# A head's RMS-norm factor: from a 128x256 square root and reciprocal to two columns of logarithm, exponential and Newton step

## The chip, the core and the metric

The kernel runs on one core of one Trainium2 chip. The metric is the device time in microseconds, the median of several executions. All times below come from the profiled execution of the kernel before, unless they are called the median of the runs.

The engines are named as in the profile: PE is TensorE, PEld its weight loads, DVE is VectorE, ACT is ScalarE, POOL is GpSimd, SP is SyncE, which issues the DMAs.

## The reference

One layer of a hybrid block over 256 latent tokens and 256 context tokens, model width 2048, all in float32. What matters here is differential attention: 8 heads, each with two query/key halves of 64 channels and 128 value channels, whose output is RMS-normalised per token over its 128 channels.

```python
def diff_attn_core(q, k, v, lam):
    s = jnp.einsum('bqhcd,bkhcd->bhcqk', q, k).astype(jnp.float32) * (ATTN_HEAD_DIM ** -0.5)
    p = jax.nn.softmax(s, axis=-1)
    a = p[:, :, 0] - lam * p[:, :, 1]
    return jnp.einsum('bhqk,bkhe->bqhe', a.astype(v.dtype), v)

def diff_attn_readout(o, subln_w, lam_init):
    B, T = o.shape[0], o.shape[1]
    return (rms_norm(o, subln_w) * (1.0 - lam_init)).reshape(B, T, ATTN_WIDTH)
```

Beside it stands a gated linear recurrence (8 heads, forward and backward) whose gates need a sigmoid, a logarithm and many exponentials. Both branches are merged, projected and added to the residual; a gated MLP with a width-3 convolution follows.

## The kernel before, in words

Channels lie on the 128 partitions and tokens on the free axis. Every product is made of three float32r products (high x high, high x low, low x high). A weight chunk of 128x1024 is loaded (`raw`, 4 buffers), rounded to `whi` by ACT (L72) and its rest put into `wlo` by DVE (L73); `mm3` (L77 to L79) and `gemm2_unit` (L126, L127) are the matmuls. So each weight chunk costs ACT and DVE about a microsecond each, beside whatever a head asks of them.

The stages follow one another: modulation and the first projections up to 145 us, attention from there to about 430 us, the recurrence to about 770 us, then merge, output projection and the MLP. In the stages of the mixers a projection for the next head is computed while the last heads are worked on: a head is a Python generator that yields the number of ticks after which its next part is to be emitted. A chunk of a context projection is 2 ticks, one of a query projection 1 tick; in attention two heads may be under way at once (`depth[0]` is 2). Ticks also feed a background job: a chunk of the modulation weights is loaded and multiplied and summed by DVE (L345).

The order that this emits is only a priority. The scheduler of the kernel language orders each engine's instructions by priority and by its own estimate of when each is ready, and this order is then fixed in the program; each engine takes its instructions strictly in turn. `keep_in_program_order` marks an instruction that must not be moved ahead of what was emitted before it on its engine.

A head in attention: `scores(0)` and `scores(1)` each make six matmuls into the PSUM tile `S` (L395; one buffer), DVE takes the maxima (L398) and scales them (L399), ACT makes two exponentials from `S` (L402). Since `S` has one buffer, the matmuls of `scores(1)` wait until both exponentials of `scores(0)` have read it. Then values and probabilities are transposed on PE into `tp` (PSUM, two buffers), the output is made into `ops[:, 0]`, ACT copies it to `o` (L438) and squares it to `osq` (L440). Two ticks later comes the norm: PE sums the squares over the channels with a matrix of ones, which spreads the sum over all partitions (L442), ACT takes the square root of 128x256 (L444), DVE the reciprocal of 128x256 (L445) and multiplies `o` by weight and factor (L446); ACT and DVE split the result into `att` (L448, L449). Only the merge, much later, reads `att`.

ACT holds one table set of functions at a time, and a load stands in the program wherever the next function is not in the set held. The square root and the exponential have different sets, so the norm of one head and the exponentials of the next load a table each. In the recurrence each head has a sigmoid (L630), a logarithm (L640) and exponentials (L522 to L525, L549), three sets.

When the last head of attention has ended, its SBUF pool is given back; the first tiles of the recurrence (`fq`, `lb`) lie in that memory and wait for it.

Of the kernel before, what the change touches and what calls it, by code (L numbers as in the profile page):

```python
# [16 lines left out]
P = 128  # L17
# [9 lines left out]
C1 = 3  # L27
BG_ATT0 = 0.5
BG_ATT, BG_REC, BG_MRG = 0.7, 0.1, 0.55
LEVELS = [1, 2, 4, 8, 16, 32, 64, 128]  # L30

_COLS = {}
# [9 lines left out]
def body(ctx, tc, cst_d, sel_d, cb_d, ccol_d, wn_d, xT_d, xc_d, lam_d, rope_d, mask_d, wm_d, wg0_d, win_d, wba_d,  # L42
# [288 lines left out]
    with ExitStack() as esa:  # L331
# [19 lines left out]
        with ExitStack() as es:  # L351
            at = es.enter_context(tc.tile_pool(name="at", bufs=1))
            aps = es.enter_context(tc.tile_pool(name="aps", bufs=1, space=PSUM))
            rope = at.tile([P, 2, T], F32, name="rope")
            dma.dma_start(rope, rope_d)

            ls = at.tile([P, 6], F32, name="ls")
            lj = at.tile([P, 64], F32, name="lj")
            lamt = at.tile([P, 256], F32, name="lamt")
            dma.dma_start(lamt, lam_d)  # L360
            for i in range(2):
                dve.scalar_tensor_tensor(lj, lamt[:, 128 * i:128 * i + 64], 1.0, lamt[:, 128 * i + 64:128 * i + 128],
                                         op0=ALU.mult, op1=ALU.mult, accum_out=ls[:, i:i + 1])
            act.activation(ls[:, 2:4], ls[:, 0:2], AF.Exp)
            dve.tensor_sub(ls[:, 4:5], ls[:, 3:4], ls[:, 2:3])
            dve.tensor_scalar_add(ls[:, 5:6], ls[:, 4:5], -LAM_INIT)
            nlam = ls[:, 5:6]
            subw = at.tile([P, 1], F32, name="subw")
            dve.tensor_scalar_mul(subw, col("subw"), 1.0 - LAM_INIT)

            shuf = [(i + 16) % 32 for i in range(32)]

            def rope_apply(out, src):
                rot = at.tile([P, T], F32, tag="rot", name="rot", bufs=2)
                dve.stream_shuffle(rot, src, shuf)
                t1 = at.tile([P, T], F32, tag="t1", name="t1", bufs=2)
                pool.tensor_tensor(t1, src, rope[:, 0, :], ALU.mult)
                pool.tensor_tensor(rot, rot, rope[:, 1, :], ALU.mult)
                dve.tensor_add(out, t1, rot)

            def head(h, kT, vr, qT):
                yield 3
                aT = at.tile([P, 2, 4, T], F32R, tag="aT", name="aT", bufs=1)
                prob = []

                def scores(m):
                    z = at.tile([P, 8], F32, tag="z", name="z", bufs=4)
                    pp = []

                    S = aps.tile([P, 2, 512], F32, tag="S", name="S")  # L390
                    c_ = slice(m * P, (m + 1) * P)
                    for i, (a, b) in enumerate(((0, 0), (0, 1), (1, 0))):
                        for c in range(2):
                            r_ = slice(64 * c, 64 * c + 64)
                            ins = pe.matmul(S[:, c], qT[r_, a, c_], kT[r_, b], start=i == 0, stop=i == 2)  # L395
                            if i or c:
                                tc.keep_in_program_order(ins)
                    dve.reduce_max(z[:, 0:2], S, axis=AX.X)  # L398
                    dve.tensor_scalar_mul(z[:, 2:4], z[:, 0:2], -0.125)  # L399
                    for c in range(2):  # L400
                        p = at.tile([P, 512], F32, tag="p", name="p", bufs=4)
                        act.activation(p, S[:, c], AF.Exp, bias=z[:, 2 + c:3 + c], scale=0.125,  # L402
                                       accum_out=z[:, 4 + c:5 + c])
                        pp.append(p)
                    dve.reciprocal(z[:, 6:8], z[:, 4:6])
                    dve.tensor_mul(z[:, 7:8], z[:, 7:8], nlam)
                    dve.tensor_scalar(pp[1], pp[1], z[:, 7:8], None, op0=ALU.mult)
                    dve.scalar_tensor_tensor(pp[0], pp[0], z[:, 6:7], pp[1], op0=ALU.mult, op1=ALU.add)
                    prob.append(pp[0])

                def turn(m):
                    tp = aps.tile([P, 4, P], F32, tag="tp", name="tp", bufs=2)
                    for i in range(4):
                        pe.transpose(tp[:, i], prob[m][:, i * P:(i + 1) * P], ident)
                    c_ = slice(m * P, (m + 1) * P)
                    act.copy(aT[:, 0, :, c_], tp)
                    dve.tensor_sub(aT[:, 1, :, c_], tp, aT[:, 0, :, c_].bitcast(F32))

                scores(0)
                yield 2  # L420
                scores(1)
                yield 2
                tp = aps.tile([P, 4, P], F32, tag="tp", name="tp", bufs=2)
                for i in range(4):
                    pe.transpose(tp[:, i], vr[:, i * P:(i + 1) * P], ident)
                vn = at.tile([P, 2, 4, P], F32R, tag="vn", name="vn", bufs=1)
                act.copy(vn[:, 0], tp)
                dve.tensor_sub(vn[:, 1], tp, vn[:, 0].bitcast(F32))
                yield 2
                turn(0)  # L430
                yield 1
                turn(1)
                yield 2
                ops = aps.tile([P, 2, T], F32, tag="o", name="ops")
                for i in range(4):
                    mm3(ops[:, 0], vn[:, 0, i], vn[:, 1, i], aT[:, 0, i], aT[:, 1, i], i == 0, i == 3)
                o = at.tile([P, T], F32, tag="o", name="o", bufs=2)
                act.copy(o, ops[:, 0])  # L438
                osq = at.tile([P, T], F32, tag="osq", name="osq")
                act.activation(osq, ops[:, 0], AF.Square)  # L440
                yield 2
                pe.matmul(ops[:, 1], ones, osq, start=True, stop=True)  # L442
                rs = at.tile([P, 2, T], F32, tag="rs", name="rs")
                act.activation(rs[:, 0], ops[:, 1], AF.Sqrt, bias=epst, scale=1.0 / P)  # L444
                dve.reciprocal(rs[:, 1], rs[:, 0])  # L445
                dve.scalar_tensor_tensor(o, o, subw, rs[:, 1], op0=ALU.mult, op1=ALU.mult)  # L446
                a = big.tile([P, 2, T], F32R, tag="ar", name=f"att{h}", bufs=16)
                act.copy(a[:, 0], o)  # L448
                dve.tensor_sub(a[:, 1], o, a[:, 0].bitcast(F32))  # L449
                att.append(a)  # L450

            for h in range(8):
                bg_rate[0] = BG_ATT0 if h < 2 else BG_ATT
                ks = in_tile(AK + h)
                kf = at.tile([P, 512], F32, tag="kf", name="kf")
                act.copy(kf[:, 256:], ks[:, 256:])
                kr = at.tile([P, T], F32, tag="qkr", name="kr", bufs=2)
                act.copy(kr, ks[:, :256])
                rope_apply(kf[:, :256], kr)
                kT = at.tile([P, 2, 512], F32R, tag="kT", name="kT", bufs=2)  # L460
                act.copy(kT[:, 0], kf)
                dve.tensor_sub(kT[:, 1], kf, kT[:, 0].bitcast(F32))

                vs = in_tile(AV + h)
                if AV + h in g0raw:
                    vr = vs
                else:
                    vr = big.tile([P, 512], F32, tag="ar", name="vr", bufs=16)
                    act.copy(vr, vs)

                qs = in_tile(AQ + h)
                qr = at.tile([P, T], F32, tag="qkr", name="qr", bufs=2)
                fold(qr, qs)
                rope_apply(qr, qr)
                qT = at.tile([P, 2, T], F32R, tag="qT", name="qT", bufs=2)
                act.copy(qT[:, 0], qr)
                dve.tensor_sub(qT[:, 1], qr, qT[:, 0].bitcast(F32))
                start(head(h, kT, vr, qT))

            in_tile_early(RFF + 1)  # L480
            in_tile_early(RFB + 1)
            in_tile_early(RI + 1)
            drain()
# [4 lines left out]
        with ExitStack() as es:  # L488
# [128 lines left out]
            for h in range(8):  # L617
# [9 lines left out]
                rqs = in_tile(RQ + h)  # L627
                fold(kkq[:, 2], rqs)
                act.copy(fq[:, 0], kkq[:, 2])
                act.activation(fq[:, 0:5], fq[:, 0:5], AF.Sigmoid)  # L630
                dve.tensor_mul(kkq[:, 2], kkq[:, 2], fq[:, 0])
                for d in range(2):
                    i_ = d * 8 + h
# [3 lines left out]
                pool.tensor_scalar(kc, f[:, :, T:], -1.0, 1.0, op0=ALU.mult, op1=ALU.add)  # L637
                dve.tensor_scalar(g, f, 2.0 ** -62, None, op0=ALU.max)
                dve.tensor_scalar(f, f, 2.0 ** 62, 1.0, op0=ALU.mult, op1=ALU.min)
                act.activation(fq[:, 1:9], fq[:, 1:9], AF.Ln)  # L640
                dve.tensor_add(g, g, f)
                for d, dst in ((1, PL[:, 0]), (0, PL[:, 1]), (1, PL[:, 2])):
                    dve.tensor_tensor_scan(dst[:, 1:], onet, g[:, d, 0:T], 0.0, op0=ALU.mult, op1=ALU.add)
# [318 lines left out]
```

## Time and profile before

| | |
|---|---|
| median of 3 runs | 1903.94 us (1903.0 to 1904.11) |
| the profiled execution, its own time | 1898.9 us |
| its span, first to last instruction | 1897.1 us |
| mean granted TensorE clock | 0.996 of full speed |
| busy: PE, DVE, ACT, POOL | 1841.9 (97%), 1354.3 (71%), 992.7 (52%), 377.6 us (20%) |

The profiled execution took 1898.9 us, 1.8 us more than its span and 5.0 us less than the median of the runs. The busy shares are means over stages that differ, and a busy PE is not PE at its peak, since the ends of matmuls are modelled. What counts for a change in one stage is the idle time of PE in that stage and what ended it.

### The profile page before, as it was taken

To read this page: it belongs to the slowest core of one execution; us is meant where nothing else is said; L and a number is where in the kernel's file an instruction comes from. 1 tells how busy PE (TensorE), PEld (TensorE's weight loads), DVE (VectorE), ACT (ScalarE), POOL (GpSimd) and SP (SyncE) were. 2 spreads that over 40 slices of the span, in tenths; PEclk is the share of its full clock that TensorE was granted. 3 is DMA by queue.
4 is the path that set the end of the run, shared out by engine and by line. 5 is a ranking of instruction groups with operands and counts; after the bars stand their busy time and mean duration, and the time that the engine had idled before them with its cause. 6 is when DMAs were issued, how large, how long until landed. Compare 5 with 4: busy or idle time off the path is not lost.

```text
span 1897.1 us, 27964 instructions
## 1 busy us (share of the span) xinstructions
PE 1841.9 (97%) x10430; PEld 1555.5 (82%) x10430; DVE 1354.3 (71%) x2130; ACT 992.7 (52%) x1501; POOL 377.6 (20%) x328
## 2 busy tenths in 40 slices
PE   7999999998999999999999999999999999999997
PEld 3777787777788888888888889888888888888886
DVE  4549878888866677977777879767677677654444
ACT  3336445447655556744444556555555555534442
POOL 0002111103223333401110110322222222211111
PEclk9999999999999999999999999999999999999998
DMA  9977665674333334688888865666666666666664
GB/s 374 370 274 248 202 197 186 207 267 145 97 111 113 110 103 122 210 269 273 280 272 272 276 192 183 192 189 190 190 188 191 188 195 187 185 193 187 192 192 123
DMA packets 112360, 385.71 MB, mean 203 GB/s; under 512 B 12384, under 2 KB 16608, under 8 KB 112224
## 3 DMA queue, kind: packets, MB, share of 16 engines
q1 hardware_dynamic: 112224, 383.92, 63.9%
q8 instruction: 82, 1.34, 0.3%
q14 instruction: 54, 0.44, 0.1%
HBM read 381.78 MB, written 2.10 MB: 202 GB/s over the span
## 4 chain that ended last, share of the span: by engine, by line
PE 72%; DMA 11%; DVE 10%; issue 4%; ACT 2%; POOL 0%; DVEq 0%; SPq 0%; ACTq 0%; POOLq 0%
PE macc L126 28%; PE macc L127 14%; DMA raw<-in_wm 8%; PE acc L126 5%; PE acc L78 4%; PE acc L79 4%; PE acc L77 4%; DVE wlo L73 3%; PE acc L127 3%; PE g L177 2%; DMA raw<-in_win 2%; DVE raw L345 2%; PE acc L177 2%; PE nat L177 2%; ACT whi L72 1%
## 5 line engine op out<-in xcount | busy, mean ns | idle before, releaser
L73 DVE TENSOR_TENSOR wlo<-raw,whi 128x1024 fp32r<-128x1024 f32 (+1 forms) x514 | 626.8, 1220 | 240.2 <-ACT whi L72 234.4
L72 ACT CAST whi<-raw 128x1024 fp32r<-128x1024 f32 (+1 forms) x514 | 530.6, 1033 | 469.9 <-PE macc L126 155.5
L126 PE MATMUL macc<-h,whi 128*128 128x512 f32 x1344 | 466.0, 391 | 0.0
L127 PE MATMUL macc<-h,wlo 128*128 128x256 f32 x1344 | 376.3, 280 | 0.0
L126 PE MATMUL acc<-h,whi 128*128 128x512 f32 x896 | 323.6, 402 | 1.1 <-DVE kkq L143 0.7
L126 PEld LDWEIGHTS macc<-h,whi 128*128 128x128 f32 x1344 | 251.3, 187 | 55.1
L127 PE MATMUL acc<-h,wlo 128*128 128x256 f32 x896 | 254.3, 284 | 6.2 <-DVE wlo L73 5.9
L127 PEld LDWEIGHTS macc<-h,wlo 128*128 128x128 f32 x1344 | 254.0, 189 | 0.0
L126 PE MATMUL macc<-f,whi 128*128 128x512 f32 x704 | 244.1, 391 | 0.0
L77 PE MATMUL acc<-h,whi 128*128 128x512 f32 x528 | 211.8, 401 | 0.0
L345 DVE SCALAR_TENSOR_TENSOR raw<-raw,cb 128x1024 f32<-128x1024 f32 x128 | 162.2, 1270 | 67.0 <-DMA raw<-in_wm 66.5
L78 PE MATMUL acc<-h,whi 128*128 128x512 f32 x528 | 207.0, 392 | 0.0
L79 PE MATMUL acc<-h,wlo 128*128 128x512 f32 x528 | 206.7, 391 | 0.0
L126 PEld LDWEIGHTS acc<-h,whi 128*128 128x128 f32 x896 | 169.1, 189 | 39.7 <-PE acc L127 1.0
L127 PE MATMUL macc<-f,wlo 128*128 128x256 f32 x704 | 197.1, 280 | 0.0
L127 PEld LDWEIGHTS acc<-h,wlo 128*128 128x128 f32 x896 | 170.0, 190 | 12.8 <-DVE wlo L73 12.2
L126 PEld LDWEIGHTS macc<-f,whi 128*128 128x128 f32 x704 | 131.6, 187 | 28.9
L842 POOL TENSOR_TENSOR u<-u 128x256 f32<-128x256 f32 x44 | 69.2, 1572 | 328.0 <-DVE u L837 288.0
L127 PEld LDWEIGHTS macc<-f,wlo 128*128 128x128 f32 x704 | 133.1, 189 | 0.0
L77 PEld LDWEIGHTS acc<-h,whi 128*128 128x128 f32 x528 | 99.2, 188 | 21.9 <-issue 2.9
L79 PEld LDWEIGHTS acc<-h,wlo 128*128 128x128 f32 x528 | 99.1, 188 | 21.5 <-issue 0.6
L78 PEld LDWEIGHTS acc<-h,whi 128*128 128x128 f32 x528 | 99.3, 188 | 20.5 <-issue 1.8
(740 smaller groups left out, 2639.0 us busy)
## 6 DMA issues: line engine op xcount, KB each, us to landing
raw<-in_win SPq DMA_DIRECT2D x178, 512.0 KB, 4.3
raw<-in_wup SPq DMA_DIRECT2D x168, 512.0 KB, 3.6
raw<-in_wm SPq DMA_DIRECT2D x128, 512.0 KB, 4.3
raw<-in_wdn SPq DMA_DIRECT2D x80, 512.0 KB, 3.7
nraw<-in_wn SPq DMA_DIRECT2D x64, 512.0 KB, 7.8
raw<-in_wout SPq DMA_DIRECT2D x32, 512.0 KB, 4.4
raw<-in_wba SPq DMA_DIRECT2D x16, 512.0 KB, 4.5
raw<-in_wbr SPq DMA_DIRECT2D x16, 512.0 KB, 4.7
```

The source lines that it names most:

```text
L72: act.copy(hi[:, :n], raw[:, :n])
L73: dve.tensor_sub(lo[:, :n], raw[:, :n], hi[:, :n].bitcast(F32))
L77: pe.matmul(ps, wh, xh, start=first, stop=False)
L78: pe.matmul(ps, wh, xl, start=False, stop=False)
L79: pe.matmul(ps, wl, xh, start=False, stop=last)
L126: pe.matmul(ps, hi[:, c_], xs[k][:, :, :T], start=k == 0, stop=False)
L127: pe.matmul(ps[:, :T], lo[:, c_], xs[k][:, 0, :T], start=False, stop=k == len(xs) - 1)
L177: tc.keep_in_program_order(pe.matmul(*args, **kw))
L345: dve.scalar_tensor_tensor(raw, raw, 1.0, cb[half], op0=ALU.mult, op1=ALU.mult, accum_out=modp[:, t - 32, half:half + 1])
L842: pool.tensor_tensor(cs[1], cs[0], cs[1], ALU.mult)
```

## The change

The norm no longer takes its factor for all 128 partitions. Two matmuls with `osq` as weights and one column of ones put the sums of squares by token: tokens on partitions, one column for each half of 128 tokens. On these 128x2 numbers DVE forms mean plus epsilon, ACT takes the logarithm and the exponential of minus half of it, and DVE makes one Newton step on the result (three small instructions). DVE then scales the identity matrix by each column, which makes two diagonal matrices; one tick later PE multiplies ones by these, which spreads the factors over all partitions into `ops[:, 1]`, and the multiplication of `o` reads them from PSUM. The 128x256 square root and reciprocal go.

Logarithm and exponential lie in one table set, which is now loaded by name: once at the start of attention, and in each head of the recurrence between its sigmoid and its logarithm. The order of ACT's table-bound instructions around these loads is kept.

```diff
+LN_EXP = "natural_log_exp_and_others"
...
+            tc.keep_in_program_order(act.preload_act_table_set(LN_EXP))
...
-            act.activation(ls[:, 2:4], ls[:, 0:2], AF.Exp)
+            tc.keep_in_program_order(act.activation(ls[:, 2:4], ls[:, 0:2], AF.Exp))
...
                 yield 2
-                pe.matmul(ops[:, 1], ones, osq, start=True, stop=True)
-                rs = at.tile([P, 2, T], F32, tag="rs", name="rs")
-                act.activation(rs[:, 0], ops[:, 1], AF.Sqrt, bias=epst, scale=1.0 / P)
-                dve.reciprocal(rs[:, 1], rs[:, 0])
-                dve.scalar_tensor_tensor(o, o, subw, rs[:, 1], op0=ALU.mult, op1=ALU.mult)
+                nt = aps.tile([P, 4, P], F32, tag="tp", name="nt", bufs=2)
+                for m in range(2):
+                    pe.matmul(nt[:, 2, m:m + 1], osq[:, m * P:(m + 1) * P], ones[:, 0:1], start=True, stop=True)
+                r = at.tile([P, 4, 2], F32, tag="r", name="r", bufs=2)
+                dve.tensor_scalar(r[:, 0], nt[:, 2, 0:2], 1.0 / P, EPS, op0=ALU.mult, op1=ALU.add)
+                act.activation(r[:, 1], r[:, 0], AF.Ln)
+                act.activation(r[:, 2], r[:, 1], AF.Exp, scale=-0.5)
+                dve.tensor_mul(r[:, 1], r[:, 2], r[:, 2])
+                dve.scalar_tensor_tensor(r[:, 1], r[:, 1], -0.5, r[:, 0], op0=ALU.mult, op1=ALU.mult)
+                dve.scalar_tensor_tensor(r[:, 3], r[:, 1], 1.5, r[:, 2], op0=ALU.add, op1=ALU.mult)
+                dg = at.tile([P, 2, P], F32, tag="osq", name="dg")
+                for m in range(2):
+                    dve.tensor_scalar(dg[:, m], ident, r[:, 3, m:m + 1], None, op0=ALU.mult)
+                yield 1
+                for m in range(2):
+                    pe.matmul(ops[:, 1, m * P:(m + 1) * P], ones, dg[:, m], start=True, stop=True)
+                dve.scalar_tensor_tensor(o, o, subw, ops[:, 1], op0=ALU.mult, op1=ALU.mult)
...
-                act.activation(fq[:, 0:5], fq[:, 0:5], AF.Sigmoid)
+                tc.keep_in_program_order(act.activation(fq[:, 0:5], fq[:, 0:5], AF.Sigmoid))
...
-                act.activation(fq[:, 1:9], fq[:, 1:9], AF.Ln)
+                tc.keep_in_program_order(act.preload_act_table_set(LN_EXP))
+                tc.keep_in_program_order(act.activation(fq[:, 1:9], fq[:, 1:9], AF.Ln))
```

## Rows read from the trace of the kernel before

**Rows 1.** Windows: attention, start and middle of the recurrence; the columns stand above.

```profile
core 0: us, PE busy (x) PEld busy (x) DVE busy (x) ACT busy (x) POOL busy (x), PEclk, DMA share, GB/s
145.00:430.00 285.00, 272.52 (x1372) 220.18 (x1371) 239.19 (x407) 143.72 (x245) 35.74 (x35) 0.99 0.68 218
430.00:500.00 70.00, 61.13 (x331) 50.62 (x330) 63.02 (x109) 51.58 (x74) 24.84 (x24) 1.00 0.40 121
500.00:740.00 240.00, 239.82 (x1237) 204.69 (x1236) 166.85 (x327) 133.63 (x182) 75.56 (x74) 1.00 0.36 108
```

**Rows 2.** PE's waits in attention: us in total, times, longest.

```profile
PE S L395 <- ACT p L402: 8.2, 7, 2.2
```

**Rows 3.** Timeline of PE, one head: start, us, line, xcount [idle before <-releaser].

```profile
312.41 0.59 PE L442 MATMUL ops<-osq,ones 128*128 128x256 f32 x2
312.94 0.96 PE L395 MATMUL S<-kT,qT 64*128 64x512 f32 x6
...
321.21 0.39 PE L79 MATMUL acc<-h,wlo 128*128 128x512 f32 x1
321.44 0.39 PE L77 MATMUL acc<-h,whi 128*128 128x512 f32 x1
323.39 0.96 PE L395 MATMUL S<-kT,qT 64*128 64x512 f32 x6 [1.57 <-ACT p L402]
```

**Rows 4.** Timeline of DVE, the same head.

```profile
316.37 1.22 DVE L398 TENSOR_REDUCE z<-S 128x2 f32<-128x1024 f32 x1
317.50 1.74 DVE L445 RECIPROCAL rs<-rs 128x256 f32<-128x256 f32 x1
319.16 0.11 DVE L399 TENSOR_SCALAR z<-z 128x2 f32<-128x2 f32 x1
...
319.51 0.48 DVE L446 SCALAR_TENSOR_TENSOR o<-o,subw,rs 128x256 f32<-128x256 f32 x1
```

**Rows 5.** Timeline of ACT, the same head.

```profile
313.49 1.28 ACT L444 ACT_TABLE_LOAD   x1
...
319.35 1.28 ACT L402 ACT_TABLE_LOAD   x1 [3.55 <-DVE z L399]
320.64 0.69 ACT L402 ACTIVATE p<-S,z 128x512 f32<-128x512 f32 x1
```

**Rows 6.** ACT's groups in attention: xcount | busy us, mean ns | idle before.

```profile
L402 ACT ACT_TABLE_LOAD x7 | 9.0, 1283 | 19.6 <-DVE z L399 19.6
L444 ACT ACT_TABLE_LOAD x7 | 9.0, 1283 | 0.1
...
L364 ACT ACTIVATE ls<-ls 128x2 f32<-128x2 f32 x1 | 0.2, 205 | 0.0
```

**Rows 7.** Timeline of PE in the first stage: matmuls of two columns.

```profile
62.45 0.50 PE L177 MATMUL nat<-sel,ns 128*128 128x2 f32 x4
62.81 0.48 PE L177 MATMUL g<-h,whi 128*128 128x512 f32 x1
```

**Rows 8.** Timeline of PE in the recurrence: float32 products of 128x128.

```profile
456.52 0.46 PE L571 MATMUL dc<-E 128*128 128x128 f32 x2 [0.68 <-DVE E L552]
456.81 0.39 PE L572 MATMUL dc<-E 128*128 128x128 f32 x2
```

**Rows 9.** DVE's groups in attention.

```profile
L445 DVE RECIPROCAL rs<-rs 128x256 f32<-128x256 f32 x8 | 14.0, 1745 | 0.0
...
L407 DVE TENSOR_SCALAR p<-p,z 128x512 f32<-128x512 f32 x16 | 8.7, 543 | 0.2
```

**Rows 10.** PE's waits in the recurrence: us in total, times, longest.

```profile
PE ktp L565 <- DVE KQ L526: 2.8, 1, 2.8
PE ktp L565 <- issue: 1.9, 1, 1.9
```

**Rows 11.** Timeline of ACT at the start of the recurrence.

```profile
425.10 0.62 ACT L626 COPY fq<-g0sb 128x512 f32<-128x512 f32 x1 [1.12 <-DVE att L449]
425.74 1.28 ACT L503 ACT_TABLE_LOAD   x1
...
442.10 1.28 ACT L640 ACT_TABLE_LOAD   x1 [0.44 <-DVE fq L639]
```

## The prediction, made before the change was run

> **What bounds the kernel now.** I read the busy time by stretch first, because the change touches two stages only [rows 1]. In attention PE is busy 272.5 of 285 us, so about 12.5 us are idle; DVE is busy 239 and ACT 144. In the first 70 us of the recurrence PE idles 8.9 us, and in the 240 us after that 0.2 us. So the later recurrence is PE's own pace: whatever ACT saves there moves nothing. All that this change can give lies in the 12.5 us of attention and the 8.9 us at the start of the recurrence, and anything it adds to PE has to be paid almost in full.
>
> The waits of PE say what the 12.5 us are [rows 2]: 8.2 us, in seven pieces of at most 2.2, are the scores' matmuls that wait for the exponentials that still read the only `S` buffer. One head shows how that comes about [rows 3 to 5]. The first scores are issued at 312.94. DVE takes their maxima at 316.37, but the scaling of these maxima (0.11 us) comes only at 319.16, because the reciprocal of the norm of the head before stands between them for 1.66 us. Then ACT, idle for 3.55 us until the scaled maxima are there, loads the table of the exponential, 1.28 us, because the square root had loaded its own at 313.49. The exponentials begin at 320.64, and the second scores, next in PE's order, begin at 323.39 after 1.57 us of idle PE. So the reciprocal and one of the two table loads lie on the path that ends in PE's wait; the other load, at 313.49, lies where ACT has slack.
>
> **The change, part by part.** The sum is made against the profiled execution's own 1898.9 us.
>
> *ACT.* Seven loads for the square root and seven for the exponential go [rows 6]; the logarithm and the exponential on two columns cost 0.205 us each, by the 128x2 exponential in the same group. That is 2.57 us less and 0.41 more per head. As total load it is worth nothing, since ACT is busy half of the stage [rows 1]; only the 1.28 us between maxima and exponentials counts.
>
> *DVE.* The reciprocal goes, 1.745 us [rows 9]. In its place come four instructions on two columns. The scaling of the maxima, of the same shape, took 0.11 us [rows 4]; I take 0.16 each, half as much again, since each waits for the result of the one before. Two more make 128x128 from the identity: between 0.11 for 2 columns and 0.54 for 512 [rows 4, 9] a straight line gives 0.22 each. Sum 1.1 us, so 0.6 less per head.
>
> *The wait of the scores.* If the new small instructions stand just where the reciprocal stood, the exponentials start 1.28 + 1.66 - 1.1 = 1.8 us sooner, which covers every wait but the longest. If a staging instruction of about 1.2 us (the length of the maxima in [rows 4]) slips between them as well, it is 0.6 us, times seven 4.3 us. The upper end is the whole 8.2. I take 6.5: nearest to the first case, with some kept back because the first heads have no norm in front of them.
>
> *PE.* The norm's matmul took 0.53 us (312.41 to 312.94, [rows 3]). Now there are two products with the squares as weights and one column to multiply. The trace has the like: two products with two columns, four passes, 62.45 to 62.81, 0.36 us [rows 7]. And two float32 products of 128x128, 0.29 us each (456.52 to 456.81, [rows 8]), 0.58. So 0.36 + 0.58 - 0.53 = 0.41 us more per head, 3.3 over eight; 2.9 if the spreading costs what the old matmul did, 4.1 if each switch costs another 0.1. PE has no slack in this stage, so all of it counts.
>
> *The new wait.* Before, nothing on PE waited for the norm. Now the spreading does, at the end of a chain PE, DVE, ACT twice, DVE five times, PE, and all later matmuls of PE, staged weights or not, queue behind it. The bare chain is 0.4 + 0.15 + 0.4 + 0.4 + 0.45, about 1.8 us, with the queues of DVE (up to two staging instructions) and ACT up to some 6. The cover is what is emitted between the two: six scores matmuls (0.96 us) and one chunk of the next projection, 24 matmuls at 0.23 (321.21 to 321.44), 5.5 us; 6.5 in all. So it is mostly covered, and the scheduler will put it later if it reckons it late. I take 0.8 us over the eight heads, with 0 and 12 (1.5 per head) as ends, because in this very stage the scheduler's estimate left the scores 1 to 2 us short.
>
> *The two other tiles.* The sums borrow a buffer of `tp` and the diagonals the buffer of `osq`. Both are free by then (the transposes of the head are over, the squares read), and read again by the next head only some six ticks later: nothing, unless the spreading is delayed by more than that cover.
>
> *Start of the recurrence.* The first tile there waits for the last head's `att` (425.10, [rows 11]), then comes the table load for the exponential of `lb`, 1.28 us, which goes since that set is already held. The load before the logarithm stood behind the wait for its operand (442.10) and may now be done ahead of it, another 1.28. PE's waits there that hang on this chain are 4.7 us [rows 10]. The last head's norm is also the release of the memory; its chain has more hops but no reciprocal and no loads. I take a gain of 2.0, with 4.7 at the good end and a loss of 3 if the longer chain of hops releases the memory later.
>
> How a load is to be priced can be read twice. In the rows it is 1.28 us and nothing more: the exponential starts at 320.64, where the load that began at 319.35 ends [rows 5]. The Trainium skill, ScalarE: Activation LUTs, What ACT_TABLE_LOAD costs, adds a drain of some 1.38 us to the 1.28, 2.66 for every change of set. By that price, an estimate, the longest wait would go too (0.4 more) and the two loads of the recurrence's start would count double (2.7 more), and the sum below would be about 3 us lower; the trace speaks against it.
>
> **Sum.** -6.5 + 3.3 + 0.8 - 2.0 = -4.4 us: 1894.5 us for an execution like the profiled one, and, as that stood 5.0 us under the median, 1899.5 us as the median. The bound of no change that can be told is 0.2%, 3.8 us.
>
> **The rivals.** *The wait only moves (0.25).* The scores no longer wait, but the spreading does, by about as much: the second scores are emitted right behind it. For it speaks that both hang on the same two queues; against it that the chain has 6.5 us of cover. -6.5 + 3.3 + 4.5 - 0.5 = +0.8: 1904.7 us.
>
> *The spreading matmul becomes a barrier (0.15).* It is the slow side: PE takes its matmuls in turn, and the scores at 323.39 show weights staged and ready matmuls standing behind one that waits [rows 3]. If the chain takes 8 us instead of 6.5 in each head, -6.5 + 3.3 + 12 = +8.8, 1912.7 us. It decides from about 1.1 us per head on (0.1 is in the forecast; 8.2 us more over eight heads make +3.8). The Trainium skill, TensorE: Matmul & The Clock Gate, Step-by-step: what each phase is for, has the same rule, that only weight loads are pulled ahead and matmuls stay in order; the trace agrees, with that 1.57 us.
>
> *All of it is won (0.15).* Scores wait no more (8.2), the spreading is hidden, and the recurrence starts without its 4.7 us: -8.2 + 2.9 - 4.7 = -10.0, 1893.9 us.
>
> *The loads stay (0.05).* If the exponentials of the scores still get a load of their own set, only reciprocal for small instructions is won: 0.56 x 7 = 3.9 against 3.3: 1903.3 us.
>
> **How the numbers follow.** The forecast has 0.40, with its own range of -8 to -1 us around -4.4, 1896 to 1903; some two thirds of it lie beyond -3.8. Faster by over 0.2%: 0.27 of it, 0.15 of all won, 0.03 of the rest, 0.45. Slower: the barrier and a little of the moved wait, 0.17. Within 0.2%: 0.38. The range of 8 in 10 goes from 1892.5, a little beyond all won, to 1908.5, between the moved wait and the full barrier.
>
> **What will show it.** Right: attention's table loads fall from 14 at scores and norm to none, the exponentials start within 1 us of the scaled maxima, PE's wait of the scores falls from 8.2 to under 2, the spreading matmuls wait under 0.3 us each, and the middle of the recurrence keeps its length although its table loads fall too. Wrong: a PE wait of over 1 us at the spreading matmul in most heads; scores that still wait a microsecond, because DVE's order puts something else between maxima and scaling; or a start of the recurrence that comes later because the last norm's hops each queue behind a staged chunk.

## The result, and the profile after

The changed kernel took 1913.17 us (median of 4 runs, 1909.81 to 1914.67) against 1903.47 us of the kernel before on the same chip: a ratio of 1.0052, 95% interval 1.0039 to 1.0065. It is slower by 0.4 to 0.65%; the forecast was 1899.5 us with a range up to 1908.5. The profiled execution has a span of 1911.0 us, 13.9 more than the one before. That is some 4 more than the difference of the medians, 9.7 us, since the profiled execution of the kernel before stood 5.0 us under its median and this one 0.4.

The page's busy times of the changed kernel:

```profile
PE 1851.3 (97%) x10478; PEld 1567.7 (82%) x10478; DVE 1352.3 (71%) x2170; ACT 969.6 (51%) x1491; POOL 382.8 (20%) x328
```

The same line of the kernel before:

```profile
PE 1841.9 (97%) x10430; PEld 1555.5 (82%) x10430; DVE 1354.3 (71%) x2130; ACT 992.7 (52%) x1501; POOL 377.6 (20%) x328
```

ACT lost its 23 us, and the time grew all the same: PE is busy 9.4 us longer and idle (span less busy) 59.7 us instead of 55.2, 4.5 more. That is the whole 13.9.

Both traces hold the same products of the projections (`acc`) in number, so, with their order taken as the same, the n-th of one can be set beside the n-th of the other. By them the changed kernel is 0.4 us ahead where the kernel before stands at 300 us and 4.4 behind at 330; between these lies the head shown below. It is 6.2 behind at 430, 11.2 behind from 520 to 790 and 13.9 at the end of the span.

Windows of the changed kernel, columns as in [rows 1]: attention, three parts of it of 15 us, and the start and middle of the recurrence.

```profile
145.00:430.00 285.00, 271.96 (x1381) 221.56 (x1380) 234.12 (x442) 120.62 (x237) 33.16 (x34) 0.98 0.66 211
165.00:180.00 15.00, 13.07 (x55) 9.82 (x53) 14.26 (x24) 6.28 (x12) 1.42 (x2) 0.89 0.85 273
315.00:330.00 15.00, 11.58 (x44) 8.63 (x44) 13.46 (x28) 4.88 (x13) 1.51 (x2) 0.77 0.44 140
390.00:405.00 15.00, 12.47 (x54) 9.47 (x53) 14.33 (x32) 5.35 (x14) 0.00 (x0) 0.89 0.78 254
430.00:500.00 70.00, 60.50 (x312) 50.89 (x311) 55.83 (x98) 51.55 (x67) 25.90 (x19) 0.94 0.41 127
500.00:740.00 240.00, 239.09 (x1232) 204.20 (x1231) 170.71 (x331) 127.03 (x182) 78.83 (x76) 1.00 0.35 106
```

The column after POOL is the granted clock. In the start of the recurrence it is 0.94 instead of 1.00. A clock of 0.77 over 15 us is 6.9 us at the lower level, 1.2 instead of 2.4 GHz (0.23 x 15 x 2); 0.94 over 70 us is 8.4. Read so all over the span up to its last 50 us, the changed kernel has some 27 us at the lower level, the kernel before 3.3. Of the 27, 13.5 lie in attention, 10.2 at the start of the recurrence and 3.3 in the merge. The middle of the recurrence takes what it took, as forecast.

PE's waits in attention, which answer to [rows 2]:

```profile
PE ops L462 <- DVE dg L459: 8.5, 4, 3.4
PE S L398 <- ACT p L405: 3.0, 2, 1.9
```

The scores wait 3.0 us instead of 8.2. The new spreading matmul (L462) waits 8.5 for the diagonal. Together they are 11.5, more than before; since other small waits went, PE idles 13.0 us in attention against 12.5 by the windows. The head at 312 us, the one of [rows 3 to 5], shows where the new wait arises. PE:

```profile
312.01 0.50 PE L449 MATMUL nt<-ones,osq 128*128 128x1 f32 x4
312.44 0.96 PE L398 MATMUL S<-kT,qT 64*128 64x512 f32 x6
...
318.68 0.39 PE L80 MATMUL acc<-h,wlo 128*128 128x512 f32 x1
322.49 1.22 PE L462 MATMUL ops<-dg,ones 128*128 128x128 f32 x4 [3.42 <-DVE dg L459]
323.64 1.65 PE L398 MATMUL S<-kT,qT 64*128 64x512 f32 x6
325.21 0.79 PE L78 MATMUL acc<-h,whi 128*128 128x512 f32 x1
```

DVE, with the norm's instructions L451 to L459:

```profile
315.66 1.23 DVE L346 SCALAR_TENSOR_TENSOR raw<-raw,cb 128x1024 f32<-128x1024 f32 x1 [4.43 <-DMA raw<-in_wm]
316.81 0.08 DVE L346 DVE_READ_ACCUMULATOR raw<-raw,cb 128x1 f32 x1
316.81 0.15 DVE L451 TENSOR_SCALAR r<-nt 128x2 f32<-128x2 f32 x1
316.89 1.22 DVE L74 TENSOR_TENSOR wlo<-raw,whi 128x1024 fp32r<-128x1024 f32 x1
318.02 0.69 DVE L454 TENSOR_TENSOR r<-r 128x2 f32<-128x2 f32 x1
318.64 1.21 DVE L401 TENSOR_REDUCE z<-S 128x2 f32<-128x1024 f32 x1
...
320.48 1.75 DVE L346 SCALAR_TENSOR_TENSOR raw<-raw,cb 128x1024 f32<-128x1024 f32 x1
322.16 0.08 DVE L346 DVE_READ_ACCUMULATOR raw<-raw,cb 128x1 f32 x1
322.16 0.47 DVE L459 TENSOR_SCALAR dg<-ident,r 128x128 f32<-128x128 f32 x2
```

The reader is to see three things. The sums are on PE from 312.01 to 312.44, but DVE stands for 4.43 us, until 315.66, at L346, a background product (the modulation weights), because that chunk's load has not landed; the norm's first instruction is behind it in DVE's order. Then the chain's small steps are each queued behind a large one: a staging subtraction, the maxima, another background product of 1.75 us. So the spreading starts 10.1 us after the sums, where PE's cover ends at 319.07 (318.68 + 0.39). Of the 10.1, 3.2 are the standing for the load (312.44 to 315.66); the rest are instructions that run. And after 3.42 us of idling PE runs at the lower clock: the spreading takes 1.22 us instead of 0.71 at 262.89, where it waited 1.72 us, the scores 1.65 instead of 0.96, a product 0.79 instead of 0.50.

Over attention DVE stands 22.8 us for such loads:

```profile
DVE raw L346 <- DMA raw<-in_wm: 22.8, 14, 4.6
```

The kernel before has the same wait, and in the same head too, so the change didn't bring it; it put a matmul of PE behind it.

```profile
DVE raw L345 <- DMA raw<-in_wm: 23.0, 17, 4.5
314.08 1.23 DVE L345 SCALAR_TENSOR_TENSOR raw<-raw,cb 128x1024 f32<-128x1024 f32 x1 [4.35 <-DMA raw<-in_wm]
```

### The profile page after: what moved, and what is told of

Read it like the earlier page. It is cut to its first block, busy times and chain, and to the rows that moved or that the text cites. A ratio compares the mean times of both kernels' runs of the same rounds, so it can differ in the third digit from the quotient of the medians.

```text
span 1911.0 us, 28075 instructions
## 1 busy us (share of the span) xinstructions
PE 1851.3 (97%) x10478; PEld 1567.7 (82%) x10478; DVE 1352.3 (71%) x2170; ACT 969.6 (51%) x1491; POOL 382.8 (20%) x328
## 4 chain that ended last, share of the span: by engine, by line
PE 59%; DMA 7%; DVE 5%; issue 2%; ACT 1%; POOL 0%; DVEq 0%; ACTq 0%; POOLq 0%
PE macc L127 28%; PE macc L128 14%; DMA raw<-in_wm 5%; PE acc L79 3%; PE acc L78 3%; PE acc L80 3%; PE acc L127 3%; DVE wlo L74 2%; PE acc L128 2%; DMA raw<-in_win 1%; PE lv L607 1%; DVE raw L346 1%; DMA raw<-in_wba 1%; ACT whi L73 1%; PE stp L598 0%
## 5 line engine op out<-in xcount | busy, mean ns | idle before, releaser
L127 PE MATMUL macc<-h,whi 128*128 128x512 f32 x1344 | 466.0, 391 | 0.0
L127 PE MATMUL acc<-h,whi 128*128 128x512 f32 x896 | 322.9, 401 | 0.0
L127 PEld LDWEIGHTS macc<-h,whi 128*128 128x128 f32 x1344 | 251.3, 187 | 55.1
L127 PE MATMUL macc<-f,whi 128*128 128x512 f32 x704 | 244.1, 391 | 0.0
L346 DVE SCALAR_TENSOR_TENSOR raw<-raw,cb 128x1024 f32<-128x1024 f32 x128 | 160.8, 1260 | 72.4 <-DMA raw<-in_wm 71.9
L127 PEld LDWEIGHTS acc<-h,whi 128*128 128x128 f32 x896 | 169.0, 189 | 37.0 <-issue 0.7
L127 PEld LDWEIGHTS macc<-f,whi 128*128 128x128 f32 x704 | 131.6, 187 | 28.9
```

Of the source, the lines that this page charges most:

```text
L127: pe.matmul(ps, hi[:, c_], xs[k][:, :, :T], start=k == 0, stop=False)
L346: dve.scalar_tensor_tensor(raw, raw, 1.0, cb[half], op0=ALU.mult, op1=ALU.mult, accum_out=modp[:, t - 32, half:half + 1])
```

## The experiments

Ratios are to the kernel before on the same chip. An expectation speaks of theory A: the spreading matmul is late, and all of PE's work behind it; B: the recurrence's half of the change costs; C: the extra matmul work on PE costs it, without any long wait; and of D, formed after the first four runs: DVE's background products, waiting in its order for their loads, delay whatever chain PE waits for.

**The two halves apart.** First the norm's new form with the recurrence as before.

> Only the norm and the table set of attention are changed; the recurrence is left as before. Of the 13.9 us by which the changed kernel's profiled span is longer, 5.6 have arisen by the last head's norm, 3.5 in the recurrence and 4.8 after it. If the late spreading matmul is the cause and the rest only follows from it (theory A): +8 to +12 us over before. If the kept order and the named load in the recurrence cost by themselves (theory B): +4 to +6 us, the attention's share alone. If the extra matmul work is the cause (theory C): +3 us, with no PE wait of over 1 us needed.

Then the recurrence's half alone:

```
-                act.activation(fq[:, 0:5], fq[:, 0:5], AF.Sigmoid)
+                tc.keep_in_program_order(act.activation(fq[:, 0:5], fq[:, 0:5], AF.Sigmoid))
...
-                act.activation(fq[:, 1:9], fq[:, 1:9], AF.Ln)
+                tc.keep_in_program_order(act.preload_act_table_set(LN_EXP))
+                tc.keep_in_program_order(act.activation(fq[:, 1:9], fq[:, 1:9], AF.Ln))
```

> Only the recurrence is changed: sigmoid, named load and logarithm in kept order; the norm of attention is as before. Theory A: no change, within 3 us of before, with fewer table loads in the recurrence. Theory B: +4 to +8 us, with PE waits of 2 to 4 us at the start of the recurrence and half clock behind them. Theory C: no change.

The norm alone: 1913.1 us, 1.0067 (1.0046 to 1.0087); the spreading matmul again waits 8.5 us. The recurrence's half alone: 1897.67 us, 0.9982 (0.9966 to 0.9997), a small gain, so B fell. All of the loss is the norm's, and it is far over the 3 us of C.

**The spreading matmul later**, `yield 3` in place of `yield 1` ahead of it.

> The changed kernel, but the spreading matmuls are emitted three ticks after the sums instead of one, behind one more chunk of a projection: about 12 us of cover instead of 6.5. Theory A: the 8.5 us of PE waits at the spreading matmuls and the half-clock stretches at about 322 and 397 us go; attention ends 2 to 5 us earlier than in the kernel before; in total 1897 to 1904 us, 9 to 16 us less than the changed kernel. Theory B: only the attention part comes back, 5 to 8 us less than the changed kernel, still slower than before by 3 to 6. Theory C: as slow as the changed kernel, within 3 us.

1906.34 us, 1.0025 (1.0013 to 1.0037): half of the loss gone. PE's waits in attention of that run:

```profile
PE S L398 <- ACT p L405: 5.7, 6, 2.1
PE ops L78 <- DVE o L463: 2.3, 2, 1.7
PE tp L417 <- DVE p L411: 2.1, 1, 2.1
```

The matmul waits no more, but the scores wait again and so do two others behind DVE. The time is the one that stood under B, which the run before had ruled out, and not that of A. The late matmul was real, and not the whole of it.

**Logarithm and exponential without the spreading.** One product with ones, as before, and the two functions on 128x256; no Newton step and no diagonal.

```
+                pe.matmul(ops[:, 1], ones, osq, start=True, stop=True)
+                act.activation(rs[:, 0], ops[:, 1], AF.Ln, bias=epst, scale=1.0 / P)
+                act.activation(rs[:, 1], rs[:, 0], AF.Exp, scale=-0.5)
```

> The changed kernel without the way by token: one matmul with ones as before, then logarithm and exponential on 128x256, the Newton step left out (the factor is a little less exact), no diagonal, nothing on PE that waits for the norm. Tables and recurrence as in the changed kernel. Theory A: PE waits of the scores fall under 2 us, no half clock from 250 us on in attention, attention ends 4 to 8 us before that of the kernel before; in total 1893 to 1900 us. Theory B: attention the same, but the recurrence loses 3 to 8 us again: about 1900 to 1906. Theory C: 3.3 us less than e3_spread_later and no more.

1902.49 us, 1.0008 (0.9996 to 1.002). This kernel has neither reciprocal nor table load in the chain of the scores, nor a matmul that waits for the norm, and gains nothing, against the 1893 to 1900 us of A. It is 3.9 us faster than the run with the late spreading, about the 3.3 that C gives to the extra matmul work. PE's waits of the scores in attention:

```profile
PE S L398 <- ACT p L405: 7.7, 8, 2.0
PE S L398 <- DVE raw L346: 2.6, 1, 2.6
```

PE and DVE around the same head:

```profile
320.32 0.39 PE L80 MATMUL acc<-h,wlo 128*128 128x512 f32 x1
323.33 1.65 PE L398 MATMUL S<-kT,qT 64*128 64x512 f32 x6 [2.62 <-DVE raw L346]
```

```profile
317.43 1.23 DVE L346 SCALAR_TENSOR_TENSOR raw<-raw,cb 128x1024 f32<-128x1024 f32 x1 [4.84 <-DMA raw<-in_wm]
```

The second scores now stand 24 products behind the first; at the head of [rows 3] it was 34. That the scheduler reckons the chain shorter and moves the scores up by as much is read from this order; the wait is the same again. DVE stands for loads longer here than in the kernel before, 31.8 us in attention against 23.0, and 4.84 us of it at this head. Theory D comes from here.

**Without the background in attention.** The first 65 of the 128 chunks, loads and products, are left out of both kernels (their sums are zero).

> The kernel before with 65 of the 128 background chunks (load, product and sum of the modulation weights) left out and none placed in attention; their sums are zero. Theory D (a background product that waits in DVE's order for its own load holds up the chain that PE waits for): the scores' wait falls from 8.2 us to under 4, and the kernel ends 5 to 10 us earlier than before, from those waits and from work of the background itself. Rival (the reciprocal and the table load are the delay): the scores still wait 7 us or more in all.

> The changed kernel with the same 65 chunks left out. Theory D: the spreading matmul's wait falls from 8.5 us to under 3, no stretch of attention falls to half clock, and this kernel lies within -2 to +4 us of the kernel before without the chunks (its extra PE work, 3.3 us, less what the scores' wait still gives). Theory A (the spreading matmul is a barrier by its own chain of hops): it still waits 1 us or more per head and this kernel is 8 to 13 us slower than the other one without chunks.

Before: 1891.76 us, 0.9942 (0.993 to 0.9954). Changed: 1892.65 us, 0.9941 (0.9927 to 0.9954). The change costs nothing any more, as D said. This takes DVE's work on the chunks out of attention together with the waits for them. PE's waits of the changed one in attention, where no spreading matmul is left, and then those of the other:

```profile
PE S L399 <- ACT p L406: 3.1, 2, 1.7
```

```profile
PE S L396 <- ACT p L403: 2.7, 3, 1.4
```

**Products behind the heads' chain**: each background product pinned in DVE's order behind the latest scaling of maxima or diagonal, the heads' parts taken first.

> The changed kernel with all its work, but each background product placed behind the latest scaling of maxima or the latest diagonal in DVE's order, and a tick runs the heads' parts ahead of the background. Theory D: the spreading matmul waits under 2 us in all, half-clock stretches in attention mostly go, and the kernel is 8 to 14 us faster than the changed one, 1899 to 1905 us. Rival A: the waits stay at 6 to 9 us and so does the time, 1910 to 1915 us.

1954.63 us, 1.0274 (1.0254 to 1.0294), a clear miss. The spreading matmul's wait did fall, to 1.6 us at the last head, but PE now waits for staged weights, at the end of attention once for 17.8 us (L127 at 461.03). By the code, a product that comes later holds its `raw` buffer longer, and staged weights take theirs from the same four; that this is the cause is argued. PE's waits for the weights up to 430 us:

```profile
PE acc L78 <- ACT whi L73: 8.9, 7, 1.8
PE acc L127 <- ACT whi L73: 6.0, 4, 1.9
```

**PE kept at work ahead of two late spreadings**, by products that compute nothing of use.

> The changed kernel with 30 and 22 matmuls of 128x256 that compute nothing of use placed just ahead of the spreading matmuls of heads 4 and 6, where PE idled 3.4 and 2.5 us. If the idling itself costs clock afterwards (about 6.8 and 3.4 us at half clock behind those two waits, 5 us of work lost), PE now works through the waits, the granted clock stays at 1.0 behind them, and the kernel is 2 to 5 us faster than the changed one although it does more: 1908 to 1911 us. Rival (the half clock has another cause or costs nothing): same time as the changed one or up to 3 us slower, 1912 to 1917 us.

1916.96 us, 1.0079 (1.0063 to 1.0095): not faster, the time that stood under the rival. Where 30 products filled the wait, PE was busy all through and the clock stayed up (0.77 in the changed kernel):

```profile
315.00:330.00 15.00, 15.00 (x85) 12.78 (x84) 12.26 (x27) 4.26 (x11) 2.57 (x2) 1.00 0.53 157
```

That fits the idling as what the clock fell for. But the filling moved the other waits (4.0 us are left at the spreadings, and PE waits 3.44 us ahead of 341.30, with 0.66 granted from 340 to 345 us), so what the clock is worth in time stays unsettled by this run.

**Background moved to the recurrence**: rates 0.15 and 0.3 in attention for 0.5 and 0.7, 0.6 in the recurrence for 0.1.

```
-BG_ATT0 = 0.5
-BG_ATT, BG_REC, BG_MRG = 0.7, 0.1, 0.55
+BG_ATT0 = 0.15
+BG_ATT, BG_REC, BG_MRG = 0.3, 0.6, 0.55
```

> The changed kernel with all its work, but the rate of background products in attention cut to less than half (0.5 and 0.7 a tick to 0.15 and 0.3) and that of the recurrence raised from 0.1 to 0.6 to make up for it. Theory D (background products waiting in DVE's order for their loads are what the spreading matmul waits for): the spreading matmul's wait falls from 8.5 us to under 5, half clock in attention to one stretch at most, and the kernel is 6 to 12 us faster than the changed one, 1901 to 1907 us. Rival A (the chain of hops alone makes the wait): wait and time stay within 3 us of the changed kernel's, 1910 to 1916 us; if the recurrence can't take the chunks, it shows there as waits of PE and the time is above 1916 us.

> The kernel before with the recurrence's half of the change and the same new rates. Theory D: the scores' wait falls from 7.1 us towards the 2.7 us of the kernel without the chunks, 1892 to 1897 us, which beats both kernels. Rival: the scores' wait is set by the reciprocal and the table load, stays at 6 to 8 us, and the time stays at 1897 to 1900 us.

> The kernel before with the new rates alone. Theory D: scores' wait under 5 us, 1896 to 1901 us. Rival: 1902 to 1906 us. Against the changed kernel with the same rates it tells what the change is worth where the background is thin: theory D says that it is within 4 us either way, theory A that the changed one is 8 us or more slower.

> The changed kernel with the new rates and the spreading matmul three ticks behind the norm's products instead of one. With both causes of the late diagonal thinned, the spreading matmul shouldn't wait at all; theory D: within 3 us of the changed kernel with the new rates, since that one has little left to win. Theory A: the later place alone brings 5 us or more.

1930.54, 1927.2, 1925.67 and 1925.94 us; 1.0148, 1.0135, 1.0124 and 1.0127, each within 0.0017. The total missed widely, and the place says why. In attention the spreading matmul's wait fell from 8.5 to this in the first, and to none in the last:

```profile
PE ops L462 <- DVE dg L459: 1.7, 2, 1.1
```

The recurrence, which PE filled before, now has such waits: DVE's for background loads from 500 to 740 us in the kernel before with these rates, and PE's waits from 520 to 800 in the changed one.

```profile
DVE raw L345 <- DMA raw<-in_wm: 30.2, 16, 3.5
```

```profile
PE lv L607 <- DVE S L610: 12.6, 5, 3.6
```

With the later place on top, the change costs 0.3 us against the kernel before with the same rates; without it 4.9. D had said within 4 us for the second, and a gain of at most 3 us from the later place: it brought 4.6, near the 5 of A, though the spreading waited only 1.7 us without it.

**Products without their loads.** The first 64 chunks are not loaded, and their products, of the same shape, take the resident tile twice.

> The changed kernel with the loads of the first 64 background chunks left out; their products are still made, of the same shape, from the resident tile with itself, so DVE's work stays and only the wait for a load goes (these sums are not those of the reference). Theory D, waiting: the spreading matmul's wait falls from 8.5 us to under 4, half clock in attention to one stretch at most, and the time from 1913 to 1898 to 1905 us. Theory D', occupancy: DVE's 80 us of products stand in the way as before, the spreading matmul waits 6 to 9 us, 1908 to 1914 us.

> The kernel before with the same loads left out and the same products kept. Theory D, waiting: the scores' wait falls from 8.2 us to 3 to 6 (the reciprocal and the table load remain in the chain), 1895 to 1901 us, and the changed kernel without these loads lies within 5 us of it. Theory D', occupancy: scores still wait 7 us or more, 1900 to 1904 us, and the changed kernel stays 8 us or more behind.

Changed: 1900.43 us, 0.999 (0.998 to 0.9999). Before: 1891.28 us, 0.994 (0.9926 to 0.9953). DVE is no less busy in attention than it was (241.3 us against 234.1), and the spreading matmul's wait is down from 8.5:

```profile
PE ops L463 <- DVE dg L460: 1.8, 2, 1.2
```

So what makes the spreading late in attention is not the time of the products. Whether it is the standing for their loads or the loads' traffic this run can't tell, since the DMA share falls with them (0.33 in attention against 0.66); the next runs keep the loads. And the kernel before gained as well, 10.5 us, so the distance between the two is still 9.1 us, where D had at most 5 and its rival 8 or more. By the n-th products of the projections, the changed profile is 1.7 us behind the other where attention begins, 5.1 at its end and 8.9 from 520 us on. So 3.8 of it arise at the start of the recurrence, which waits 3.8 us at `ktp` and then has this window:

```profile
475.00:490.00 15.00, 11.18 (x48) 9.52 (x47) 13.94 (x23) 8.15 (x15) 3.42 (x3) 0.77 0.32 106
```

**Products behind the weights loaded after them.** A chunk's product is placed behind the staging subtraction of the weights whose load was issued next, so it can hardly find its load missing. First for all chunks:

```
+            los.append(dve.tensor_sub(lo[:, :n], raw[:, :n], hi[:, :n].bitcast(F32)))
...
+                    held.append((t, half, raw, len(los)))
...
+                    if k < len(los):
+                        tc.add_manual_dep(ins.ins, los[k].ins.name,
```

> The changed kernel with all its work, and each background product placed in DVE's order behind the staging subtraction of the weights that were loaded next after its chunk. If the order alone is the cause, DVE's waits for background loads fall from 22.8 us in attention to under 8, the spreading matmul's wait from 8.5 to under 4, and the time to 1900 to 1907 us. If the loads' traffic was the cause, or the buffers held longer starve the staging of weights (as with products put behind the heads' chain), PE waits for staged weights and the time stays above 1910 us.

> The kernel before with the recurrence's half of the change and the same placing of the background products. If the order alone is the cause: the scores' wait falls from 7.1 us to 3 to 5 and the time to 1891 to 1896 us, which beats all kernels with the whole work so far. If not: 1898 us or more, with PE waiting for staged weights.

1921.88 us, 1.0099 (1.0084 to 1.0113), and 1921.06 us, 1.0091 (1.0075 to 1.0107). DVE's wait for background loads in attention of the first fell from 22.8 to 2.8 us and that of the spreading matmul to 5.6, where under 4 was expected; its recurrence ended 9 us sooner, but the merge lost more, to weights staged late. PE's waits of the first from 800 to 1100 us:

```profile
PE acc L130 <- DVE wlo L76: 9.9, 17, 0.8
```

Then for the first 64 chunks alone, `if half == 0 and k < len(los)`:

> The changed kernel with only the first 64 background products (those of attention) placed behind the weights loaded after them; the merge keeps its order. Theory D: the merge takes what it took before, the gain of 9 us at the end of the recurrence stays, 1901 to 1907 us. Rival (the order moves the loss on to wherever it is next paid): 1910 us or more.

> The kernel before with the recurrence's half of the change and the same placing of the first 64 products. With all products placed so its recurrence ended 2.7 us later than without (794.7 against 792.0 us), from one wait of 4.2 us for staged weights at 410 us: so 1898 to 1902 us, no gain over the recurrence's half alone. Theory D in its pure form, without that wait: 1891 to 1896 us.

Changed kernel: 1899.37 us, 0.9988 (0.9976 to 0.9999), with all of its work. Recurrence's half: 1899.99 us, 0.9996 (0.9987 to 1.0006). The page of the first, and its waits of DVE for the loads and of PE for the diagonal in attention:

```profile
PE 1845.9 (97%) x10478; PEld 1563.3 (82%) x10478; DVE 1352.3 (71%) x2170; ACT 964.7 (51%) x1488; POOL 390.3 (21%) x328
```

```profile
DVE raw L348 <- DMA raw<-in_wm: 4.4, 5, 1.4
PE ops L468 <- DVE dg L465: 6.9, 2, 5.3
```

Its span is 1900.1 us, so PE idles 54.2 us, less than before the change, and is busy 4.0 us longer. This placing of 64 instructions is worth 0.64% of the time, 12 us, the ratio 1.0052 against 0.9988. With it the norm's new form costs nothing (0.9988 against the 0.9996 of the recurrence's half), where it cost 0.67% by itself. The spreading matmul still waits 6.9 us in all. But 5.25 of them fall on the last head, where three background products end after the sums have begun at 406.18, the last of them after 1.28 us for its load; in the heads before it the wait is 1.6 us instead of 8.5. The wait at the last head was not tried further. Some 10 us at the lower clock are left, all from 405 to 420 us, instead of 27. Of kernels with the whole work this one and the recurrence's half alone are the fastest; their intervals overlap.

## Why the prediction was wrong

*The new wait, taken at 0.8 us, is the step that failed.* It measured 8.5, and 10.2 us at the lower clock followed two of its four pieces. The working set a bare chain of 1.8 us, "with the queues up to some 6", against 6.5 us of cover. At 312 us the chain took 10.1 us. I had counted DVE's queue as up to two staging instructions; at that head it held one that stood for its load, then a staging subtraction, the maxima and a second background product. The view was at hand: 23.0 us of DVE's waits in attention were for background loads, and I read PE's waits only.

*The scores' wait* fell by 5.2 us, near the 6.5 taken, but it seems not for the reason given. In the run without the spreading the shorter chain brought no gain, and at the head shown the scores were moved up by ten products. The term took the order of PE as fixed while the change re-makes it. At that head the scores stand right behind the spreading, which waits in their place; with the spreading later they waited 5.7 us again. That this holds for every head was not looked at.

*PE's work*, taken at 3.3 us, is some 4, an estimate: the norm's products last 0.43 us (312.01 to 312.44) and the spreading 0.64 at the full clock (359.30 to 359.94, scores next), against 0.53. The pages can't settle it, since busy time holds the clock too: PE is busy 4.1 us longer in the version with the first 64 products placed behind the weights than in its counterpart with the recurrence's half, 2.5 longer without loads and 6.7 longer without chunks. Right in kind.

*The start of the recurrence*, taken at -2.0, is the second term that failed: it came out at +5.0 (6.2 us behind at 430, 11.2 at 520). The recurrence's half alone gave 3.4 us, 0.6 to 6.5 by its interval; of the 3.6 in its profile at the end of the recurrence, 1.2 arose at its start and 2.4 ahead of it. In the changed kernel the granted clock there is 0.94. PE's waits that answer to [rows 10] did not shrink:

```profile
PE ktp L582 <- DVE KQ L543: 3.8, 1, 3.8
PE lv L607 <- POOL E L569: 2.0, 1, 2.0
```

The load before the logarithm went ahead of its operand, as forecast: ACT around it in the changed kernel.

```profile
431.18 1.28 ACT L647 ACTIVATE fq<-fq 128x1280 f32<-128x1280 f32 x1
432.36 1.03 ACT L73 CAST whi<-raw 128x1024 fp32r<-128x1024 f32 x1
433.41 1.28 ACT L657 ACT_TABLE_LOAD   x1
...
438.00 1.92 ACT L658 ACTIVATE fq<-fq 128x2048 f32<-128x2048 f32 x1 [1.97 <-DVE fq L656]
```

*DVE's small instructions*, taken at 1.1 us a head, are 1.5: 155, 360, 153 and 155 ns, and twice 341 for the diagonals. What they last was not what mattered. Of the signs named, no table load is left at scores and norm in attention, and the exponentials shown start 0.26 us after the scaled maxima (320.24 to 320.50); but the scores wait 3.0 us and not under 2, and the spreading waits over 1 us in three heads of eight.

*The account.* The sum had attention at -2.4 us (-6.5 + 3.3 + 0.8), the start of the recurrence at -2.0 and the rest at nothing; by the n-th products of the projections they are +6.2 (from the start of the span), +5.0 and +2.7. By PE, 13.9 us = 4.0 of its work + 4.5 of idling + the 5.4 left of the 9.4 that it is busy longer. The last I put down to the clock: 24 us more at the lower level could cost 12 if PE had worked through all of them. That split is argued from the rows; no run isolated it. The sum had no term for the clock at all.

*The rivals.* The barrier had the right shape and by chance nearly the right time, 1912.7 us. Its price was a chain of 8 us in each head, 12 us of waits; the wait was 8.5, in four heads, and the same hops wait 1.8 us without the loads and no longer at all without the chunks. The Trainium skill, TensorE: Matmul & The Clock Gate, Step-by-step: what each phase is for, has matmuls stay in order; the 3.42 us in which PE did nothing ahead of L462 agree.

*What stays open.* That DVE's queue makes the spreading late is shown; that this lateness is the whole loss is not. Without loads the spreading waits 1.8 us and the change still costs 9.1, while without chunks it costs nothing and with the new order nothing either. Why the recurrence starts worse in some of these orders was not found; the scheduler re-makes all queues at every edit, and two runs never differ in one place only.

## What to carry to other kernels

Before a chain is given to PE to wait for, look at who else stands in the queues that it passes, and what those wait for: a large optional instruction that waits for its own load holds up everything behind it, however short the chain. Where a scheduler sets the order from its own estimate, shortening a chain that PE waits for can move the consumer up by as much and win nothing. To take background work out of the way, one can place it behind work that needs a later load; here that paid for the chunks of attention and lost in the merge, where weights were then staged late.

## What was not expected of the hardware

Behind some of PE's waits the granted clock fell from its upper level, 2.4 GHz, to its lower, 1.2: 0.77 over 315 to 330 us behind 3.42 us of idling, 0.89 over 390 to 405 behind 2.53, and 0.89 over 165 to 180 behind 1.93 us for which the scores waited. The spreading and the scores then took 1.7 times as long (1.22 against 0.71, 1.65 against 0.96 us). Behind other waits of that length it stayed at 1.00: 2.76 us ahead of 487.44 in the kernel before, 2.08 ahead of 169.51 in the version with the first 64 products placed behind the weights. So the length of a wait alone doesn't say whether the clock falls, and what does stays open.

The price can be read at 322.49. From there the spreading, the scores and six products take 5.41 us, to 327.90. The same pieces at the full clock take about 3.0, an estimate from the rows: the spreading 0.64 (359.30 to 359.94), the scores 0.89 (312.44 to 313.33), six products 1.49 (313.33 to 314.82). So this wait of 3.42 us cost some 2.4 us more behind it, and a forecast that counted waits alone came out too low.
